# One-hot gate products with the first key as a copied, dense stationary operand, and the weights on the second key

## The chip, the cores and the metric

The kernel runs on one core of one Trainium2 chip. The metric is the device time of one execution in microseconds; the time before is the median of three runs. Engine names in the profile are PE (TensorE products), PEld (TensorE weight loads), DVE (VectorE), ACT (ScalarE), POOL (GpSimd) and SP (SyncE, which issues the DMAs).

## What is computed

The reference is one forward pass of two blocks on 256 tokens of width 1024. The last part is a layer of 16384 experts, addressed by product keys: 128 first keys times 128 second keys. Each token has 8 heads, and each head picks 16 experts, so a token has 128 pairs (first key, second key) with a weight each. Cut to what matters:

```python
# per token n: i1, i2 (128 picks each) and softmax weights g (128)
# G[n, a, b] = sum over picks of g * (i1 == a) * (i2 == b)
# y[n] = sum over a, b of G[n, a, b] * gelu(h[n] . u[a, b]) * v[a, b]
```

The kernel computes G for all 16384 experts of a token as a product of matrices on TensorE: the picks lie on the 128 partitions, one operand is the one-hot matrix of the first keys (128 picks x 128 keys), the other that of the second keys, and one of the two is multiplied by the weights. The weights are held in two fp16 parts (a high and a low one), so each token takes two products that add up in PSUM.

## The kernel before, in words

`peer` holds the layer. After the scores of the keys and the choice of the best 16 per head (`topk`), `weights` (line 1560) leaves the picks' first keys, second keys, weights' high part and low part transposed in `it` [128 picks, 4, 256 tokens], fp16. The loop over 64 expert chunks `c` (line 1618) multiplies the tokens' activations with two groups of 128 columns of `pu` per chunk (`gemm_t_chunk`, by way of `mm3`, lines 211 to 213: three products of 256 columns for each of 16 steps, all from float32r operands in two parts). Each group's weights are loaded by DMA to `raw`, copied by ScalarE to `whi` (line 206) and subtracted by VectorE to `wlo` (line 207), with three buffers each. The GELU of the result goes into `A` (lines 1637 to 1640).

From chunk 31 on (`GSTART`), the loop also calls `group` for four tokens at a time (`NT`), 64 groups over 33 chunks. `group` keeps `AHEAD` = 2 groups prepared by `spread` (line 1589). `spread` makes two tiles on VectorE, tokens innermost:

- `o` [128 picks, 2 keys, 128 values, 4 tokens]: a ramp `iof` compared with the keys (line 1594);
- `ow` [128 picks, 2 parts, 128 values, 4 tokens]: the first key's one-hot times the two weight parts (line 1595).

`group` then issues eight products (line 1607), for each token two, with `ow` of one part as the stationary operand and the second key's one-hot in `o` as the moving one. Both are read with a step of four values, since the tokens are innermost. The result [128 first keys, 128 second keys] of a token lands in a PSUM tile `t` of four buffers. VectorE multiplies it into the part of `A` that is done (line 1610), and ScalarE copies the rest into `A` (line 1612). The pool `oh` of `o` and `ow` has three buffers for each. The order on each engine is set by a scheduler with a cost model of its own, within the dependences. Afterwards the loop over `pv` multiplies `A` with the experts' outputs.

Of the kernel before, what the change touches and what calls it, by code (L numbers as in the profile page):

```python
# [43 lines left out]
def layout(inp):  # L44
    """Input arrays in the order in which the chip reads them: copies and zero padding only."""
# [16 lines left out]
    a = {}  # L62
# [90 lines left out]
class Builder:  # L153
# [19 lines left out]
    # ---------------------------------------------------------------- helpers  # L173
# [25 lines left out]
    def wchunk(self, src):  # L199
        """A chunk of weights in two exact float32r parts."""  # L200
        n = src.shape[-1]
        raw = self.wp.tile([128, n], F32, name="raw", bufs=self.raw_bufs)
        self.D.dma_start(raw, src)
        hi = self.wp.tile([128, n], F32R, name="whi")
        lo = self.wp.tile([128, n], F32R, name="wlo")
        self.S.activation(hi, raw, AF.Copy)  # L206
        self.last_lo = self.V.tensor_sub(lo, raw, hi.bitcast(F32))  # L207
        return hi, lo
# [8 lines left out]
    def warm(self, n, after=None):  # L217
        """Keeps TensorE's clock up while it waits: n products that nobody reads."""
# [11 lines left out]
    def gemm_n(self, act, src, evac, blocks=None, split=None, chunks=None):  # L230
        """Tokens on partitions, blocks of 512 features; chunks: the part of the contraction; split: the chunks in
        groups that all blocks take in turn."""
# [20 lines left out]
    def gemm_t(self, act, src, g, out, first):  # L253
        """One group of 128 features on partitions, [128, 256 tokens]."""
# [5 lines left out]
    def gemm_t_chunk(self, act, src, filling=False):  # L260
        """Two groups; filling: both follow the rows of an operand that is still being filled."""
# [12 lines left out]
    def order(self, first, then):  # L274
        """On one engine, then is issued after first."""
# [8 lines left out]
    def rsqrt(self, a):  # L284
        """a ** -0.5 on [128, n] float32, in place of a: a first guess from the bits, three Newton steps."""
# [16 lines left out]
    def fill(self, act, x, gain, ks=range(8), bias=None, k0=0):  # L302
        """x [128 tokens, 2, features] to features on partitions, times gain (plus bias), in two parts."""
# [21 lines left out]
    def square(self, x, acc, scale=1.0 / 32):  # L325
        """acc: the sum of (scale x) ** 2."""
        self.last_sq = self.S.activation(self.junk[:, 0:x.shape[-1]], x, AF.Square, scale=scale, accum_out=acc)

    def row_r(self, ss):
        """The rows' 1 / rms from two halves' sums, [128, 2 tiles, 2 halves] to [128, 2]."""  # L330
# [5 lines left out]
    def row_b(self, r, dst):  # L336
        """The rows' factors along the free axis, on all partitions, [128, 256]."""
# [24 lines left out]
    def norm_act(self, act, x, ss, gain, bias, pool):  # L362
        """Rows over their rms, times gain plus bias."""
# [11 lines left out]
    # ---------------------------------------------------------------- first block  # L375
# [15 lines left out]
    def add_x(self, ss):  # L391
        """Adds a product to x and takes the sums of squares."""
# [6 lines left out]
    def mixer1(self):  # L399
        nc, V, S, T, P = self.nc, self.V, self.S, self.T, self.P  # L400
        with self.pool("m1") as mp, self.pool("ss") as ssp, self.pool("cv") as cvp, self.pool("sbt") as sbp:
# [8 lines left out]
            with self.pool("a1") as ap:  # L410
# [56 lines left out]
                # the branches' products, each with its rows' factors  # L467
# [10 lines left out]
    def stick_pre(self, q, r, sq, sp):  # L478
        """Queries and keys, normed, a pair of heads on partitions."""
# [25 lines left out]
    def stick(self, qt, v, m, sq, sp):  # L505
        V, S, T, P = self.V, self.S, self.T, self.P
        self.act_table("natural_log_exp_and_others", self.last_s)
        # keys on partitions: masked where key >= query
# [46 lines left out]
        def end():  # L555
            """The rows' 1 / rms."""
# [10 lines left out]
    def conv_sum(self, ab, cp):  # L567
        """The depthwise convolution: the first taps on VectorE, the last on TensorE as diagonal products."""
# [63 lines left out]
    def ssm_pre(self, sp, ends):  # L632
# [13 lines left out]
        # cos and sin of theta * t, [128 states, 8, 256], t from 1 (the phase of step t is t-1 later)  # L646
# [12 lines left out]
        # discretisation  # L659
# [16 lines left out]
        # inputs' weights, a group's channels to its states; outputs' weights times the inputs' factor fr + i fi  # L676
# [21 lines left out]
    def ssm(self, u, ab, mixed, sums, sp, mag, cs, sn, pad, bl):  # L698
        V, S, T, P = self.V, self.S, self.T, self.P
        # inputs of the states, turned back by theta t, scanned, turned forth  # L700
# [44 lines left out]
    def xa_mem(self):  # L745
        """The memory, features on partitions, and its rows' 1 / rms."""
# [11 lines left out]
    def xa_k(self, q):  # L758
        """Keys of the memory."""
# [10 lines left out]
    def xa_v(self):  # L770
        """Values of the memory."""
# [4 lines left out]
    def xa_q(self, act, w, r, q):  # L776
        """Queries or keys of rows still without their factor r, and the heads' mean squares."""
# [12 lines left out]
    def xa_r(self, ss, r):  # L790
        """The heads' factors."""
# [106 lines left out]
    # ---------------------------------------------------------------- second block  # L898
    def mod(self, mp, f0, f1, after):
        """The modulation's columns: silu(c) w_mod + b_mod, [128, 48]; the context's first two parts, [128, 16]."""  # L900
# [43 lines left out]
    def gates_rows(self):  # L944
        """The modulation's last four parts as rows in DRAM."""
# [7 lines left out]
    def gate_row(self, i, dst):  # L953
        """Part i of those four on all partitions, [128, 1024]."""
# [3 lines left out]
    def mix_consts(self):  # L958
# [4 lines left out]
        # resets of the scans along tokens  # L963
# [8 lines left out]
        # keys on partitions: direction 0 keeps s <= t, direction 1 s >= t  # L972
# [20 lines left out]
    def prep_gates(self, o, act, lat, mp, tp):  # L993
        """mLSTM's gates from the projections of h (tokens of the latents or of the context)."""
        V, S, T, P = self.V, self.S, self.T, self.P
        n = "l" if lat else "c"
        # gates
# [4 lines left out]
        # log sigmoid of the forget gates, to the input gates' rows: direction 0 at 0, direction 1 at 32  # L1002
# [11 lines left out]
        def by_step(t, x, end=True):  # L1014
            """Two columns: the chunks of 128 tokens in the direction's order, or back in the tokens' order."""
# [58 lines left out]
    def prep_gla(self, o, act, lat, mp, tp):  # L1074
        """GLA's queries, keys and decays, by head: (direction, 64 channels) on partitions."""
# [4 lines left out]
        # decays' logarithms, times 16  # L1080
# [30 lines left out]
        else:  # L1111
            # down to the context's end
# [31 lines left out]
    def prep_ml(self, o, act, lat, mp):  # L1144
        """mLSTM's queries and keys: channels on partitions, convolved over three tokens."""
# [43 lines left out]
    def out_gates(self, act, gates, i):  # L1189
        """The gates on a mixer's outputs [128, 2, 512]."""  # L1190
# [83 lines left out]
    def gla_ctx(self, o):  # L1274
        """The state after the context, [128 (direction, 64 keys), head, 128 values]: a direction's first."""
# [9 lines left out]
    def gla_states(self, o):  # L1285
        """The states at the starts of the chunks of 64 tokens."""
# [504 lines left out]
```

## Time and profile before

| what | us |
|---|---|
| median of 3 runs | 1547.19 |
| lowest, highest run | 1546.6, 1550.41 |
| span of the profiled execution | 1549.8 |
| PE busy in that span | 1495.7 |
| DVE busy | 1305.8 |
| ACT busy | 824.7 |
| PE busy, 947 to 1187 us | 240.0 |
| DVE busy, 947 to 1187 us | 218.36 |
| ACT busy, 947 to 1187 us | 103.97 |

The profile is one execution on the chip. Busy time counts the instructions of an engine; a wait is put down to the instruction that ended it. Weight loads overlap products, so PE and PEld do not add up. "Idle before" in a group of instructions is the time that the engine stood still just ahead of them. The stretch from 947 to 1187 us holds the 512 products of line 1607.

### The profile page before, as it was taken

The numbers are of one execution on the slowest core, as the hardware profiler recorded it, in microseconds if no ns is written. First come the engines' busy times: TensorE is split into PE (matmuls) and PEld (weight loads), VectorE is DVE, ScalarE is ACT, GpSimd is POOL, SyncE is SP. The second block draws the span as 40 slices with busy tenths as digits, with TensorE's granted clock in tenths as the row PEclk, the third lists the DMA queues.
The fourth block names the chain that finished last, engine by engine and source line by source line (L and its number), as shares of the span: only waits on it lengthen the run. The fifth ranks groups of instructions, "written<-read, shape, count | busy, mean of one in ns | idle before, by whom it ended". The sixth has DMA issues, their size and how long they took to land.

```text
span 1549.8 us, 24779 instructions
## 1 busy us (share of the span) xinstructions
PE 1495.7 (97%) x9395; PEld 1331.7 (86%) x9395; DVE 1305.8 (84%) x2452; ACT 824.7 (53%) x1245; POOL 27.0 (2%) x34
## 2 busy tenths in 40 slices
PE   7998899999989999999999999999999999999996
PEld 7876677899977898879999999999999877887785
DVE  8989885899877767877998988888998787888788
ACT  7564666454445756645444445444444555556553
POOL 3000000000000000000000000000000000000001
PEclk9989999999999999999999999999999999999998
DMA  6630375588884553335555554444444665665553
GB/s 231 205 108 14 127 255 196 188 273 305 308 293 141 178 163 100 124 116 164 181 182 182 178 181 153 140 141 137 138 142 143 211 215 197 197 203 196 191 192 122
DMA packets 77655, 275.56 MB, mean 178 GB/s; under 512 B 8512, under 2 KB 10976, under 8 KB 76896
## 3 DMA queue, kind: packets, MB, share of 16 engines
q1 hardware_dynamic: 77536, 273.98, 53.6%
q8 instruction: 73, 1.20, 0.3%
q14 instruction: 46, 0.38, 0.1%
HBM read 271.84 MB, written 2.11 MB: 177 GB/s over the span
## 4 chain that ended last, share of the span: by engine, by line
PE 67%; DVE 15%; DMA 11%; issue 3%; ACT 3%; SPq 0%; ACTq 0%; DVEq 0%
PE g L212 17%; PE g L213 17%; PE g L211 17%; DMA raw<-in_pv 5%; PE t L1607 4%; DVE wlo L207 4%; DMA wmod<-in_w_mod 2%; ACT whi L206 2%; PE t L212 2%; PE t L213 1%; PE t L211 1%; DMA raw<-in_ffn_out 1%; DVE wmod L921 1%; DMA cc<-in_rows 1%; DVE tlo L1670 1%
## 5 line engine op out<-in xcount | busy, mean ns | idle before, releaser
L206 ACT ACTIVATE whi<-raw 128x1024 fp32r<-128x1024 f32 x420 | 443.8, 1059 | 502.4 <-PE g L212 160.3
L207 DVE TENSOR_TENSOR wlo<-raw,whi 128x1024 fp32r<-128x1024 f32 x420 | 511.2, 1221 | 112.2 <-ACT whi L206 110.0
L211 PE MATMUL g<-h2h,whi 128*128 128x256 f32 x1152 | 329.2, 286 | 0.2 <-ACT whi L206 0.2
L212 PE MATMUL g<-h2l,whi 128*128 128x256 f32 x1152 | 326.5, 284 | 0.0
L213 PE MATMUL g<-h2h,wlo 128*128 128x256 f32 x1152 | 325.4, 283 | 0.0
L211 PEld LDWEIGHTS g<-h2h,whi 128*128 128x128 f32 x1152 | 220.9, 192 | 0.8 <-ACT h2h L319 0.4
L212 PEld LDWEIGHTS g<-h2l,whi 128*128 128x128 f32 x1152 | 220.3, 191 | 0.0
L213 PEld LDWEIGHTS g<-h2h,wlo 128*128 128x128 f32 x1152 | 220.0, 191 | 0.0
L212 PE MATMUL g<-wlo,ah 128*128 128x512 f32 x328 | 126.0, 392 | 0.9 <-DVE wlo L207 0.8
L213 PE MATMUL g<-whi,al 128*128 128x512 f32 x328 | 122.9, 389 | 0.0
L211 PE MATMUL g<-whi,ah 128*128 128x512 f32 x328 | 103.3, 389 | 0.0
L211 PE MATMUL g<-hfh,whi 128*128 128x256 f32 x352 | 100.0, 285 | 3.3 <-ACT whi L206 1.9
L212 PE MATMUL g<-hfl,whi 128*128 128x256 f32 x352 | 99.5, 283 | 0.0
L213 PE MATMUL g<-hfh,wlo 128*128 128x256 f32 x352 | 98.2, 284 | 0.9 <-DVE wlo L207 0.9
L212 PEld LDWEIGHTS g<-wlo,ah 128*128 128x128 f32 x328 | 61.6, 188 | 16.1 <-DVE wlo L207 2.3
L211 PEld LDWEIGHTS g<-whi,ah 128*128 128x128 f32 x328 | 61.6, 188 | 12.9
L213 PEld LDWEIGHTS g<-whi,al 128*128 128x128 f32 x328 | 61.6, 188 | 12.6
L211 PEld LDWEIGHTS g<-hfh,whi 128*128 128x128 f32 x352 | 66.4, 189 | 5.1 <-ACT whi L206 3.2
L921 DVE SCALAR_TENSOR_TENSOR wmod<-wmod,cc 128x1024 f32<-128x1024 f32 x48 | 58.6, 1220 | 10.1 <-DMA wmod<-in_w_mod 8.2
L213 PEld LDWEIGHTS g<-hfh,wlo 128*128 128x128 f32 x352 | 65.6, 188 | 1.3 <-DVE wlo L207 1.2
L212 PEld LDWEIGHTS g<-hfl,whi 128*128 128x128 f32 x352 | 66.2, 188 | 0.0
L1607 PE MATMUL t<-o,ow 128*128 128x128 f16 x512 | 65.8, 297 | 0.0
(637 smaller groups left out, 3053.9 us busy)
## 6 DMA issues: line engine op xcount, KB each, us to landing
raw<-in_pu SPq DMA_DIRECT2D x128, 512.0 KB, 3.9
raw<-in_pv SPq DMA_DIRECT2D x128, 512.0 KB, 4.0
wmod<-in_w_mod SPq DMA_DIRECT2D x48, 512.0 KB, 5.7
raw<-in_ffn_in SPq DMA_DIRECT2D x44, 512.0 KB, 5.5
raw<-in_ffn_out SPq DMA_DIRECT2D x22, 512.0 KB, 4.5
raw<-in_w_out SPq DMA_DIRECT2D x16, 512.0 KB, 3.5
raw<-in_pwq SPq DMA_DIRECT2D x16, 512.0 KB, 4.1
raw<-in_w_qkv SPq DMA_DIRECT2D x12, 512.0 KB, 4.3
```

What stands on the lines that cost most here:

```text
L206: self.S.activation(hi, raw, AF.Copy)
L207: self.last_lo = self.V.tensor_sub(lo, raw, hi.bitcast(F32))
L211: a = self.T.matmul(out, ahi, bhi, start=start, stop=False, skip_group_check=True)
L212: self.T.matmul(out, ahi, blo, start=False, stop=False, skip_group_check=True)
L213: b = self.T.matmul(out, alo, bhi, start=False, stop=stop, skip_group_check=True)
L921: i = V.scalar_tensor_tensor(o, w, 1.0, cc[:, j], op0=OP.mult, op1=OP.mult, accum_out=acc)
L1607: T.matmul(p[:, k], w[:, i, :, k], o[:, 1, :, k], start=k + i == 0, stop=i == 1, skip_group_check=True)
L1670: V.tensor_sub(lo[:, 0:n], raw[:, 0:n], hi[:, 0:n].bitcast(F32))
```

## The change

The roles of the two keys are exchanged, and the layouts with them. `iof` shrinks to pairs of tokens. `it` holds the two keys and `wt` the two weight parts, both as [128 picks, 128 token pairs, 2, 2 tokens]. In `spread`, `o` and `ow` are [128 picks, 2 pairs, 2 keys or parts, 128 values, 2 tokens], so that two tokens are innermost. `ow` is now the second key's one-hot times the weights. ScalarE copies the first key's one-hot from `o` to a new tile `od` [128 picks, 4 tokens, 128 values], where the 128 values of one token lie side by side. The product takes `od` as the stationary operand for both parts and `ow` as the moving one, with a step of two values. `o` has two buffers in place of three. The rest of the diff removes comments.

```diff
-            self.iof = pc.tile([128, 128, NT], F16, name="iof")
-            P.iota(self.iof, pattern=[[1, 128], [0, NT]], base=0, channel_multiplier=0,
+            self.iof = pc.tile([128, 128, 2], F16, name="iof")
+            P.iota(self.iof, pattern=[[1, 128], [0, 2]], base=0, channel_multiplier=0,
...
-            it = pc.tile([128, 4, 256], F16, name="idxT")
+            it, wt = (pc.tile([128, 128, 2, 2], F16, name=n) for n in ("idxT", "wgtT"))
...
-                        V.tensor_copy(it[:, i], p)
+                        V.tensor_copy(it[:, :, i], p.rearrange("p (a t) -> p a t", t=2))
...
                         V.tensor_scalar(g, p, 32768.0, None, op0=OP.mult)
-                        V.tensor_copy(it[:, 2], g)
-                        V.tensor_sub(it[:, 3], g, it[:, 2])
+                        g = g.rearrange("p (a t) -> p a t", t=2)
+                        V.tensor_copy(wt[:, :, 0], g)
+                        V.tensor_sub(wt[:, :, 1], g, wt[:, :, 0])
...
             def spread(t0):
-                o = op[0].tile([128, 2, 128, NT], F16, name="o")
-                w = op[0].tile([128, 2, 128, NT], F16, name="ow")
-                row = lambda i: it[:, i:i + 2, None, t0:t0 + NT].to_broadcast([128, 2, 128, NT])
-                V.tensor_tensor(o, self.iof[:, None].to_broadcast([128, 2, 128, NT]), row(0), op=OP.is_equal)
-                V.tensor_mul(w, o[:, 0:1].to_broadcast([128, 2, 128, NT]), row(2))
-                ready.append((o, w))
+                n = [128, NT // 2, 2, 128, 2]
+                o = op[0].tile(n, F16, name="o", bufs=AHEAD)
+                w = op[0].tile(n, F16, name="ow")
+                d = op[0].tile([128, NT, 128], F16, name="od")
+                row = lambda z: z[:, t0 // 2:(t0 + NT) // 2, :, None].to_broadcast(n)
+                V.tensor_tensor(o, self.iof[:, None, None].to_broadcast(n), row(it), op=OP.is_equal)
+                V.tensor_mul(w, o[:, :, 1:2].to_broadcast(n), row(wt))
+                S.activation(d.rearrange("p (g t) j -> p g t j", t=2), o[:, :, 0].rearrange("p g j t -> p g t j"),
+                             AF.Copy)
+                ready.append((d, w))
...
-                o, w = ready.pop(0)
+                d, w = ready.pop(0)
...
-                        T.matmul(p[:, k], w[:, i, :, k], o[:, 1, :, k], start=k + i == 0, stop=i == 1,
+                        T.matmul(p[:, k], d[:, k], w[:, k // 2, i, :, k % 2], start=k + i == 0, stop=i == 1,
```

## Rows read from the trace of the kernel before

**Rows 1.** The page: busy time of each engine; the chain that ended last, by line.
```profile
PE 1495.7 (97%) x9395; PEld 1331.7 (86%) x9395; DVE 1305.8 (84%) x2452; ACT 824.7 (53%) x1245; POOL 27.0 (2%) x34
...
PE g L212 17%; PE g L213 17%; PE g L211 17%; DMA raw<-in_pv 5%; PE t L1607 4%; DVE wlo L207 4%; DMA wmod<-in_w_mod 2%; ACT whi L206 2%; PE t L212 2%; PE t L213 1%; PE t L211 1%; DMA raw<-in_ffn_out 1%; DVE wmod L921 1%; DMA cc<-in_rows 1%; DVE tlo L1670 1%
```

**Rows 2.** Line 1607 by itself: its weight loads and its products.
```profile
L1607 PEld LDWEIGHTS <-ow x512: 112/117/136, 947.5 to 1185.2; 128*128 128x128 f16 x171
L1607 PE MATMUL t<-o,ow x512: 282/297/303, 947.5 to 1185.3; 128*128 128x128 f16 x171
```

**Rows 3.** TensorE in order of time, 1046 to 1056 us: start, length, line, count.
```profile
1046.80 2.05 PE L1607 MATMUL t<-o,ow 128*128 128x128 f16 x16
...
1054.33 0.28 PE L213 MATMUL g<-h2h,wlo 128*128 128x256 f32 x1
1054.45 2.05 PE L1607 MATMUL t<-o,ow 128*128 128x128 f16 x16
1056.25 0.37 PE L211 MATMUL g<-h2h,whi 128*128 128x256 f32 x1
```

**Rows 4.** Busy time of the engines in four stretches of the stage: PE, PEld, DVE, ACT, POOL.
```profile
947.00:1007.00 60.00, 60.00 (x504) 59.48 (x504) 51.19 (x73) 27.79 (x47) 0.00 (x0) 1.00 0.43 136
1007.00:1067.00 60.00, 60.00 (x504) 59.49 (x503) 53.44 (x70) 26.94 (x48) 0.00 (x0) 1.00 0.42 139
1067.00:1127.00 60.00, 60.00 (x504) 59.42 (x503) 55.76 (x70) 24.41 (x47) 0.00 (x0) 1.00 0.42 139
1127.00:1187.00 60.00, 60.00 (x504) 59.42 (x503) 57.97 (x69) 24.83 (x48) 0.00 (x0) 1.00 0.43 141
```

**Rows 5.** Groups by line, 947 to 1186 us: busy, mean ns, idle before them.
```profile
L207 DVE TENSOR_TENSOR wlo<-raw,whi 128x1024 fp32r<-128x1024 f32 x63 | 77.1, 1224 | 17.2 <-ACT whi L206 16.9
L206 ACT ACTIVATE whi<-raw 128x1024 fp32r<-128x1024 f32 x63 | 67.0, 1064 | 133.7 <-issue 96.3 <-PE g L212 37.4
...
L1610 DVE TENSOR_TENSOR A<-A,t 128x256 f32<-128x256 f32 (+31 forms) x62 | 60.9, 1026 | 0.0
...
L1595 DVE TENSOR_TENSOR ow<-o,idxT 128x1024 f16<-128x1024 f16 x61 | 41.5, 688 | 0.0
L1594 DVE TENSOR_TENSOR o<-iof,idxT 128x1024 f16<-128x1024 f16 x61 | 40.9, 690 | 4.6 <-PE t L1607 4.2
```

**Rows 6.** Line 526 by itself, a product of 16-bit operands that lie dense.
```profile
L526 PEld LDWEIGHTS <-identb x16: 95/98/151, 93.6 to 138.4; 128*128 128x128 bf16 x16
L526 PE MATMUL t<-sbmask,identb x16: 219/219/314, 93.6 to 138.5; 128*128 128x128 bf16 x16
```

**Rows 7.** TensorE in order of time near 93 us: two products of line 526.
```profile
93.56 0.28 PE L526 MATMUL t<-sbmask,identb 128*128 128x128 bf16 x2
```

**Rows 8.** Lines 1513 and 1514 by themselves: VectorE on 1024 fp16 values.
```profile
L1513 DVE TENSOR_TENSOR tkz<-io,tkc x8: 673/692/696, 742.0 to 928.6; 128x1024 f16<-128x1024 f16 x8
...
L1514 DVE TENSOR_TENSOR tkz<-tkz,tkf x8: 1217/1219/1225, 744.3 to 930.8; 128x1024 f16<-128x1024 f16 x8
```

**Rows 9.** All engines in order of time, 940 to 948 us: the first groups are prepared.
```profile
940.28 1.89 DVE L1594 TENSOR_TENSOR o<-iof,idxT 128x1024 f16<-128x1024 f16 x3
...
941.74 0.58 ACT L1640 ACTIVATE A<-g 128x512 f32<-128x512 f32 x1
...
943.88 1.90 DVE L1595 TENSOR_TENSOR ow<-o,idxT 128x1024 f16<-128x1024 f16 x3
```

**Rows 10.** All engines in order of time, 1055 to 1062 us: one chunk.
```profile
1055.74 1.49 DVE L1594 TENSOR_TENSOR o<-iof,idxT 128x1024 f16<-128x1024 f16 x2
...
1059.35 1.06 ACT L206 ACTIVATE whi<-raw 128x1024 fp32r<-128x1024 f32 x1 [2.81 <-issue]
...
1060.31 0.39 ACT L1640 ACTIVATE A<-g 128x280 f32<-128x280 f32 x1
...
1062.10 0.41 PE L1607 MATMUL t<-o,ow 128*128 128x128 f16 x2
```

**Rows 11.** Line 206 by itself: ScalarE's queue waiting ahead of it.
```profile
L206 ACTq EVENT_SEMAPHORE  x62: 2382/2781/4287, 949.5 to 1180.8; - x62
```

## The prediction

> **What bounds the kernel now.** The page comes first. TensorE is busy for 97% of the span and VectorE for 84%, and in the chain that ended last the one-hot products (line 1607) have 4%, about 62 us [rows 1]. So a shorter line 1607 can matter, if nothing stands close behind TensorE where it runs. Its products start between 947.5 and 1185.2 us [rows 2], in 32 batches, one per expert chunk from chunk 31 on (the first one covers two chunks), 7.65 us apart in mid-stage [rows 3]. I call 947 to 1187 us the stage. Cut into four stretches of 60 us [rows 4], it shows TensorE full in each at a granted clock of 1.00 (its 2.4 GHz level), while VectorE climbs: 51.2, 53.4, 55.8 and 58.0 us of 60. The climb is line 1610, which grows with the chunk [rows 5]. ScalarE has 104 of 240 us. VectorE's idle time there is nearly all a wait for `whi` [rows 5], so it waits for weights that TensorE's own pace releases. TensorE bounds the stage, with VectorE 15% behind at its start and 3% behind at its end.
>
> **TensorE's part of the change.** In mid-stage a batch of 16 products starts at 1054.45, the next product of line 211 at 1056.25 [rows 3]: 1.80 us, or 112 ns per product (117 ns inside the batch, the weight load's length [rows 2]). Both operands there are read with a step of four fp16 values, 8 bytes. The nearest product with both operands dense is line 526, also 128x128 in 16 bits: 219 ns against 297, its load 98 against 117 ns [rows 2, 6], and a pair of them takes 0.28 us, so the second starts 60 ns after the first [rows 7]. The change makes the stationary operand dense and leaves the moving one a step of two fp16 values, 4 bytes. No row shows that step in 16 bits. The products of lines 211 to 213 move elements of 4 bytes side by side, 256 columns every 0.12 us [rows 3], which is 60 ns for 128. So what the array must fetch at a 4-byte pitch comes at full pace, and I take 60 ns, the value on which both rows agree. The bounds are 98 ns (loads that do not overlap, from line 526's load) and 112 ns (nothing gained). At 60 ns the saving on TensorE is 512 x 0.0525 = 26.9 us, or 6.7 us in each stretch. The number of loads and products stays: the whole span has as many loads as products [rows 1], though lines 211 and 212 share their stationary operand, so one shared by two products is loaded twice.
>
> The Trainium skill speaks against half of this. "SBUF — State Buffer" (Door 1: The DMA port swizzle, its note on cachelines) says that two hits on a 16-byte line already give full bandwidth; an 8-byte step in fp16 has two. "TensorE: Matmul & The Clock Gate" (Weight-path perf modes) lets the fast weight load read packed or strided. By these the old layout cost nothing, and that is the rival of no gain below; the 78 ns between lines 1607 and 526 speak against them here. The second page (Back-to-back issue gap) also gives 81 ns as the sustained pace at 128 columns. By it the saving on TensorE would be 512 x 0.0315 = 16 us, and the run would come out some 3 us above my number.
>
> **VectorE's part.** Per group, `o` and `ow` stay two instructions of 1024 fp16 values. Now they take 690 and 688 ns with an innermost run of four tokens [rows 5]; afterwards the run is a pair. Line 1513, with a run of 16, takes 692; line 1514, where an operand has an innermost step of zero, 1219 for the same shape [rows 8]. So the price of a pair lies between 0.69 and 1.22 us. I take 0.69, because the pair is still two adjacent values of every operand, as in line 1513 and not in 1514. The upper end is a rival. Lines 1610 and 1638 and the weights are untouched. In `weights` three casts of 256 values get outputs with gaps, once; even at the 0.69 us of four times as many values they would be 2 us, and they stand ahead of the stage, where VectorE does not set the pace.
>
> **ScalarE's part.** 64 copies of 512 values are new. The nearest row is line 1640, 128x512 in 0.58 us [rows 9]: 37 us on ScalarE, 141 of some 226. It sits idle 133.7 us before line 206 [rows 5], which covers them. What is queued behind a copy is the next `whi`; the copy waits for `o`. What waits for the copy is TensorE's batch. In a sample chunk the two `o` end at 1057.23 and the batch comes at 1062.10 [rows 10]: 4.9 us for two copies of 0.58. If they stand behind the `whi` that runs from 1059.35 and the 0.39 us after it, they end at 1061.9, with 0.2 us to spare; ahead of that `whi` they fall into its wait of 2.81 us. I cost them at nothing; without that cover the price is the rival of the late copy. The 4.2 us that `o` waits for TensorE [rows 5] go, since TensorE no longer reads `o`. At the stage's start `ow` follows 1.7 us after the last `o` [rows 9], time enough for its copies. The smaller iota is on POOL, which has 27 us of work in the whole span [rows 1].
>
> **The sum.** TensorE would need 60 - 6.7 = 53.3 us per present stretch. VectorE needs 51.2, 53.4, 55.8 and 58.0, and takes over in the last three. If it could run without a gap, the stage would be 53.3 + 53.4 + 55.8 + 58.0 = 220.5, a saving of 19.5 us. The fullest stretch that the trace shows has it at 58.0 of 60, or 96.6%. At that fill the four are 53.3, 55.3, 57.7 and 60.0, together 226.3: a saving of 13.7 us. I take the second, as it is the fill that a row shows: 14 us, half of what TensorE sheds. What is late next is VectorE, not the products. The profiled span of 1549.8 becomes 1536; it stands 2.6 us above the median of 1547.2, within the runs' 1546.6 to 1550.4, so the median becomes 1533.
>
> **Rivals.**
> - *The load sets the pace.* The product alternates with a load, and if loads of 98 ns [rows 6] do not overlap, the saving is 512 x 0.0145 = 7.4 us, TensorE stays the bound, 1540. For it: the 117 ns pace equals the load's length now. Against it: the second product of line 526 starts 60 ns after the first.
> - *No gain on TensorE.* The 112 ns come from something other than the steps, or a 4-byte step is as slow as an 8-byte one. Then 1547, give or take 3. Against it: the 78 ns and the 4-byte columns of line 211.
> - *The late copy.* ScalarE works in order, and its waits ahead of `whi` have a median of 2.8 us and reach 4.3 [rows 11]. A copy behind a long one misses the 0.2 us above, and TensorE waits. At 14 / 32 = 0.44 us per chunk the gain is gone; at 1 us per chunk the run is at 1533 + 32 = 1565, and about 1550 between.
> - *Slower: a pair breaks VectorE's pace.* If an innermost run of two drops `o` and `ow` to line 1514's 1.22 us, VectorE gets 128 x 0.53 = 68 us more: 286 us, at 96.6% 296 against 240, and the run is at 1603. It decides from 22 us on, that is, once the two take 0.86 us each. Against it: a run of four shows no loss against a run of 16.
>
> **How the numbers follow.** Forecast 0.62, with 1528 (no gap in VectorE) to 1538 as its own range; load-bound 0.13; no gain 0.10; late copy 0.08; broken pair 0.07. A measurement of this kernel tells about 0.3% (4.6 us) from no change. Faster by more: 0.62 + 0.13 + 0.01 of the late copy = 0.76. Within: 0.10 + 0.02 = 0.12. Slower: 0.07 + 0.05 = 0.12. The range from 1527 to 1549 takes in the forecast (0.59), the load-bound case (0.13), most of no gain (0.08) and a little of the late copy (0.02).
>
> **What would show it.** Right: products at line 1607's successor that start some 60 ns apart and last near 219 ns; VectorE at 96% or more of the stage from its second quarter on; TensorE with gaps for the first time there, released by `wlo` or by the copies; the stage some 226 us long; `o` and `ow` still 0.69 us. Wrong: starts 98 ns or more apart, `o` or `ow` above 0.86 us, or gaps in TensorE that end with the copy. The sum fails most easily in VectorE's fill, which no row shows without TensorE holding it back.

## The result, and the profile of the changed kernel

| | before | changed |
|---|---|---|
| median, us | 1547.04 | 1527.76 |
| lowest, highest run | 1546.6, 1550.41 | 1525.51, 1530.05 |
| span of the profiled execution | 1549.8 | 1524.2 |

The ratio is 0.9869, with a 95% interval of 0.985 to 0.9887: 20 us less, where the prediction said 14. Of the median of before 1547.2, a factor of 0.9869 is 1526.9, just under the low end of the range. A second timing, further down, gives 0.9858. So the direction was right and the gain is about one and a half times the forecast.

The page of the changed kernel, busy time of each engine and the chain by line, as in [rows 1]:

```profile
PE 1465.9 (96%) x9395; PEld 1300.3 (85%) x9395; DVE 1300.9 (85%) x2452; ACT 861.3 (57%) x1309; POOL 27.3 (2%) x34
...
PE g L211 16%; PE g L213 16%; PE g L212 16%; DMA raw<-in_pv 8%; DVE wlo L207 5%; DMA wmod<-in_w_mod 3%; ACT whi L206 2%; PE t L1614 2%; DVE tlo L1677 1%; DVE al L1667 1%; DMA raw<-in_ffn_in 1%; DVE wlo L1677 1%; PE t L212 1%; PE t L213 1%; PE t L211 1%
```

TensorE is busy 30 us less and VectorE 5 us less, ScalarE 37 us more. In the chain the one-hot products fall from 4 to 2%, and the loads of `pv` and `wlo` grow.

The products by themselves, now line 1614, to be read against [rows 2]:

```profile
L1614 PEld LDWEIGHTS <-od x512: 94/96/101, 937.1 to 1148.6; 128*128 128x128 f16 x171
L1614 PE MATMUL t<-ow,od x512: 217/219/233, 937.1 to 1148.6; 128*128 128x128 f16 x171
```

A product takes 219 ns in place of 297, its load 96 in place of 117, the same two numbers as line 526 in [rows 6]. The eight bytes' step is gone from both. Two rows in order of time at the start of the stage (start, length, engine, line, count):

```profile
933.72 1.29 DVE L1600 TENSOR_TENSOR ow<-o,wgtT 128x1024 f16<-128x1024 f16 x2
...
937.07 1.10 PE L1614 MATMUL t<-ow,od 128*128 128x128 f16 x16
```

Sixteen products take 1.10 us; less the last one's 0.22, the other fifteen start 59 ns apart. In [rows 3] the same sixteen took 2.05 us. The row above it shows two neighbouring `ow` on VectorE in 1.29 us: with 0.68 for the second, the first holds the engine for only 0.61.

The engines in stretches of the stage, as in [rows 4] (PE, PEld, DVE, ACT, POOL; the last stretch has 38 us):

```profile
937.00:997.00 60.00, 60.00 (x575) 59.53 (x575) 58.77 (x86) 42.98 (x73) 0.00 (x0) 1.00 0.49 157
997.00:1057.00 60.00, 60.00 (x568) 59.61 (x567) 58.51 (x78) 41.20 (x70) 0.00 (x0) 1.00 0.48 156
1057.00:1117.00 60.00, 60.00 (x570) 59.44 (x570) 60.00 (x75) 35.85 (x68) 0.00 (x0) 1.00 0.46 151
1117.00:1155.00 38.00, 35.86 (x334) 35.02 (x333) 37.58 (x44) 19.32 (x40) 0.00 (x0) 1.00 0.41 137
```

TensorE now gets 575, 568 and 570 products done in 60 us where it did 504, and is still full in the first three stretches. VectorE is at 58.8, 58.5, 60.0 and 37.6 of 38. The prediction's best fill, 58.0 of 60, is passed from the first stretch on.

The groups by line from the first batch to the last, as in [rows 5] (busy, mean ns, idle before them):

```profile
L207 DVE TENSOR_TENSOR wlo<-raw,whi 128x1024 fp32r<-128x1024 f32 x61 | 74.2, 1216 | 0.7 <-ACT whi L206 0.6
L206 ACT ACTIVATE whi<-raw 128x1024 fp32r<-128x1024 f32 x61 | 64.5, 1058 | 15.7 <-PE g L212 9.3 <-issue 4.3 <-DMA raw<-in_pu 0.6
L1617 DVE TENSOR_TENSOR A<-A,t 128x256 f32<-128x256 f32 (+30 forms) x60 | 58.3, 1013 | 0.0
L1600 DVE TENSOR_TENSOR ow<-o,wgtT 128x1024 f16<-128x1024 f16 x62 | 40.2, 685 | 2.0 <-PE t L1614 1.7
L1599 DVE TENSOR_TENSOR o<-iof,idxT 128x1024 f16<-128x1024 f16 x61 | 39.8, 684 | 0.0
...
L1601 ACT ACTIVATE od<-o 128x512 f16<-128x512 f16 x61 | 35.6, 618 | 0.0
```

`o` and `ow` take 684 and 685 ns, so a pair of tokens innermost costs VectorE nothing. The new copy, line 1601, takes 618 ns, with no idle time ahead of it. VectorE's 17.2 us of waiting for `whi` are 0.7 us now.

Where the time came from is best seen by cutting at the last batch. The kernel before, from the first batch to the last and the 30 us after that:

```profile
947.50:1185.30 237.80, 237.80 (x1992) 235.62 (x1991) 216.66 (x277) 103.23 (x187) 0.00 (x0) 1.00 0.43 139
1185.30:1215.30 30.00, 30.00 (x158) 25.85 (x157) 22.55 (x30) 15.34 (x23) 0.00 (x0) 1.00 0.55 176
```

And the changed one:

```profile
937.10:1148.60 211.50, 210.45 (x1998) 208.44 (x1997) 208.79 (x275) 136.25 (x243) 0.00 (x0) 1.00 0.47 153
1148.60:1178.60 30.00, 26.46 (x135) 22.45 (x133) 21.29 (x24) 14.90 (x23) 0.00 (x0) 0.94 0.51 167
```

From the first to the last batch 237.8 us become 211.5, which is 26.3 us less. In it VectorE stands still for 237.8 - 216.7 = 21.1 us before and 2.7 us afterwards. In the 30 us that follow, TensorE has no gap before, and 3.5 us of gaps afterwards. There a part is given back. The mean granted clock of that stretch is 0.94 in this profile: some 3.4 us at the lower of its two levels (1.2 GHz), behind the gaps, which costs TensorE some 1.7 us of work at the upper one.

The stretches do not hold exactly the same work. Without its 512 one-hot products, the one before has 1480 products of `pu`, the changed one 1486, and one of these takes 0.12 us [rows 3]; a difference of 1 us between two runs' batches can come from that.

### The profile page after: what moved, and what is told of

Read it like the earlier page. It is cut to its first block, busy times and chain, and to the rows that moved or that the text cites. A ratio compares the mean times of both kernels' runs of the same rounds, so it can differ in the third digit from the quotient of the medians.

```text
span 1524.2 us, 24941 instructions
## 1 busy us (share of the span) xinstructions
PE 1465.9 (96%) x9395; PEld 1300.3 (85%) x9395; DVE 1300.9 (85%) x2452; ACT 861.3 (57%) x1309; POOL 27.3 (2%) x34
## 4 chain that ended last, share of the span: by engine, by line
PE 57%; DVE 19%; DMA 14%; issue 5%; ACT 4%; SPq 0%; ACTq 0%; DVEq 0%
PE g L211 16%; PE g L213 16%; PE g L212 16%; DMA raw<-in_pv 8%; DVE wlo L207 5%; DMA wmod<-in_w_mod 3%; ACT whi L206 2%; PE t L1614 2%; DVE tlo L1677 1%; DVE al L1667 1%; DMA raw<-in_ffn_in 1%; DVE wlo L1677 1%; PE t L212 1%; PE t L213 1%; PE t L211 1%
## 5 line engine op out<-in xcount | busy, mean ns | idle before, releaser
L1617 DVE TENSOR_TENSOR A<-A,t 128x248 f32<-128x248 f32 (+31 forms) x64 | 63.3, 1032 | 0.5 <-ACT A L1647 0.5
```

The source lines that it names most:

```text
L1617: V.tensor_mul(a[:, :, 0:j0], a[:, :, 0:j0], p[:, :, 0:j0])
```

## The experiments

Two numbers of each run tell most: the stretch from the first one-hot product to the last (first and last start by the product's own line), and the rest of the span after it.

| run | first, last product | batches | span | rest |
|---|---|---|---|---|
| before | 947.5, 1185.3 | 237.8 | 1549.8 | 364.5 |
| before_again | 944.6, 1182.4 | 237.8 | 1548.3 | 365.9 |
| changed | 937.1, 1148.6 | 211.5 | 1524.2 | 375.6 |
| after_again | 939.8, 1151.3 | 211.5 | 1522.3 | 371.0 |
| after_timed | 948.8, 1160.4 | 211.6 | 1529.5 | 369.1 |
| stationary_step2 | 942.7, 1155.9 | 213.2 | 1524.0 | 368.1 |
| moving_step4 | 942.5, 1179.8 | 237.3 | 1545.9 | 366.1 |
| pairs_only | 945.8, 1159.0 | 213.2 | 1526.3 | 367.3 |
| moving_step1 | 938.7, 1152.9 | 214.2 | 1523.5 | 370.6 |
| stationary_step4 | 945.6, 1159.7 | 214.1 | 1531.1 | 371.4 |
| no_weighting | 941.7, 1152.9 | 211.2 | 1518.1 | 365.2 |
| weighting_plus_half | 944.7, 1179.3 | 234.6 | 1543.0 | 363.7 |
| low_part_on_ACT | 942.2, 1158.7 | 216.5 | 1529.7 | 371.0 |
| some_wlo_on_POOL | 942.9, 1154.9 | 212.0 | 1525.8 | 370.9 |

### Both kernels once more

No edit.

> The kernel before once more, for the spread of its parts between executions. Two theories of the 9.8 us that the loop over pv takes longer in the changed kernel's profile (368.4 against 358.6 us from the last product of pu to the end), and of the 9.7 us by which that profile is ahead when the first batch comes (937.1 against 947.5). Spread of executions: a second profile of the kernel before differs from the first by some 5 to 10 us in either part. Caused by the change: the second profile has the first batch within 2 us of 947.5 and the loop over pv within 2 us of 358.6.

> The changed kernel once more. Spread: the first batch and the loop over pv move by several us against the first profile (937.1 and 368.4), while the batches take 211 to 212 us from the first to the last product again, as that stretch is paced by TensorE. Caused by the change: 937 and 368 again, within 2 us.

The start of the first batch moves by several us from one execution to the next: 947.5 and 944.6 in the kernel before, 937.1, 939.8 and, in the third profile, 948.8 in the changed one. So the 9.7 us by which the first profile was ahead there are spread. The batches do not move: 237.8 and 237.8, 211.5, 211.5 and 211.6. The rest moves by less than the difference of the two kernels: 364.5 and 365.9 against 375.6, 371.0 and 369.1. Neither theory held for the rest as it was put. Of the 9.8 us in the first pair of profiles some is spread, but the means, 365.2 before and 371.9 in the changed kernel, leave 6.7 us for the change. Then 26.3 - 6.7 = 19.6 us is the net gain, near the 20 us of the timing.

Of the 6.7 us only a part repeats. The 30 us behind the last batch, in after_again and after_timed:

```profile
1151.30:1181.30 30.00, 26.45 (x141) 22.59 (x139) 22.64 (x26) 14.90 (x23) 0.00 (x0) 1.00 0.53 175
```

```profile
1160.40:1190.40 30.00, 26.49 (x141) 22.62 (x139) 22.62 (x26) 15.71 (x24) 0.00 (x0) 1.00 0.54 175
```

The 3.5 us of gaps are there each time. The lower clock is not: it is 1.00 in these two, with 141 products done against 135 in the first profile. So 1.7 us of the first profile's 375.6 are its clock, and in the third, 369.1, hardly anything is given back beyond the gaps.

### Which operand's step set the pace

Without ScalarE's copy, the stationary operand read straight from `o`, which has three buffers again, as in all the runs below without the copy:

```diff
-                o = op[0].tile(n, F16, name="o", bufs=AHEAD)
+                o = op[0].tile(n, F16, name="o")
...
-                d = op[0].tile([128, NT, 128], F16, name="od")
...
-                S.activation(d.rearrange("p (g t) j -> p g t j", t=2), o[:, :, 0].rearrange("p g j t -> p g t j"),
-                             AF.Copy)
-                ready.append((d, w))
+                ready.append((o, w))
...
-                        T.matmul(p[:, k], d[:, k], w[:, k // 2, i, :, k % 2], start=k + i == 0, stop=i == 1,
+                        T.matmul(p[:, k], o[:, k // 2, 0, :, k % 2], w[:, k // 2, i, :, k % 2], start=k + i == 0, stop=i == 1,
```

> The changed kernel without ScalarE's copy: the stationary operand is read straight from o with a step of two values (4 bytes), the moving one as before with a step of two. Theory A (the moving operand's 8-byte step set the old pace, the load hides): product pace stays near 58 ns and the time is that of the changed kernel within 0.3%. Theory B (the stationary operand's step set the pace, which is why a copy is needed): the load grows from 96 ns towards 117 and the pace to 75 ns or more, 512 x 0.017 = 9 us or more on TensorE's stage.

Its loads and products by themselves:

```profile
L1611 PEld LDWEIGHTS <-o x512: 96/97/101, 942.7 to 1155.8; 128*128 128x128 f16 x171
L1611 PE MATMUL t<-ow,o x512: 217/218/233, 942.7 to 1155.9; 128*128 128x128 f16 x171
```

Load and product are those of the changed kernel, 97 and 218 ns, and the ratio to the kernel before is 0.9872 (0.9832 to 0.9911), against 0.9869. So the copy brings nothing that the time shows. The batches alone are 1.7 us longer without it, 213.2 us against 211.5, with 3.4 us of gaps of TensorE in place of 1.1.

The other half: the copy and the exchanged keys, but tokens four innermost as before.

```diff
-                o = op[0].tile([128, 2, 128, NT], F16, name="o")
+                o = op[0].tile([128, 2, 128, NT], F16, name="o", bufs=AHEAD)
                 w = op[0].tile([128, 2, 128, NT], F16, name="ow")
...
-                V.tensor_mul(w, o[:, 0:1].to_broadcast([128, 2, 128, NT]), row(2))
-                ready.append((o, w))
+                d = op[0].tile([128, NT, 128], F16, name="od")
+                V.tensor_mul(w, o[:, 1:2].to_broadcast([128, 2, 128, NT]), row(2))
+                S.activation(d, o[:, 0].rearrange("p j t -> p t j"), AF.Copy)
+                ready.append((d, w))
...
-                        T.matmul(p[:, k], w[:, i, :, k], o[:, 1, :, k], start=k + i == 0, stop=i == 1,
+                        T.matmul(p[:, k], d[:, k], w[:, i, :, k], start=k + i == 0, stop=i == 1,
```

> The kernel before with the roles of the keys exchanged and ScalarE's copy, tokens still four innermost: the stationary operand dense, the moving one with the old step of four values (8 bytes). Theory A (moving step sets the pace): pace 105 to 118 ns as before, stage 230 to 238 us, time within 0.3% of the kernel before. Theory B (stationary step sets it): pace 58 to 65 ns, products of 219 ns, and the time of the changed kernel.

```profile
L1609 PEld LDWEIGHTS <-od x512: 96/115/118, 942.5 to 1179.7; 128*128 128x128 f16 x171
L1609 PE MATMUL t<-ow,od x512: 273/294/296, 942.5 to 1179.8; 128*128 128x128 f16 x171
```

With a dense stationary operand the product still takes 294 ns, the batches take 237.3 us, and the ratio is 1.0 (0.9982 to 1.0018). Theory A holds on both sides: the moving operand's step sets the pace. The load's median is 115 ns here although its operand is dense, and its shortest, 96, is the dense length, so the load's length followed the products there and did not set their pace.

Then the token pairs alone, without copy and without exchange of the keys (against the changed kernel, the lines of the copy left out):

```diff
-                V.tensor_mul(w, o[:, :, 1:2].to_broadcast(n), row(wt))
+                V.tensor_mul(w, o[:, :, 0:1].to_broadcast(n), row(wt))
...
-                        T.matmul(p[:, k], d[:, k], w[:, k // 2, i, :, k % 2], start=k + i == 0, stop=i == 1,
+                        T.matmul(p[:, k], w[:, k // 2, i, :, k % 2], o[:, k // 2, 1, :, k % 2], start=k + i == 0, stop=i == 1,
```

> Only the token pairs of the change: tokens two innermost in o and ow, but the roles as in the kernel before (ow of the first key stationary, the second key's one-hot moving) and no copy by ScalarE. Theory A (the moving operand's step is all that counts): pace 57 to 59 ns and the time of the changed kernel within 0.3%. Theory B (the exchange of the keys or the dense stationary operand adds to it): slower than the changed kernel by 0.5% or more.

```profile
L1611 PEld LDWEIGHTS <-ow x512: 95/97/101, 945.8 to 1158.9; 128*128 128x128 f16 x171
L1611 PE MATMUL t<-o,ow x512: 217/218/233, 945.8 to 1159.0; 128*128 128x128 f16 x171
```

Again 97 and 218 ns. The ratio is 0.9882 (0.9857 to 0.9908), on the same chip as 0.9858 (0.983 to 0.9887) for the changed kernel: 0.24% apart, with intervals that overlap for the most part. That is what theory A allows; theory B's 0.5% would be at the far end of the interval. In the profile its batches take 213.2 us, as those of the other kernel without the copy. Of the three parts of the change, the token pairs do the work.

Two steps that the change doesn't use. The moving operand dense:

```diff
-                        T.matmul(p[:, k], d[:, k], w[:, k // 2, i, :, k % 2], start=k + i == 0, stop=i == 1,
+                        T.matmul(p[:, k], d[:, k], d[:, k], start=k + i == 0, stop=i == 1,
```

> The changed kernel with the copied one-hot od as the moving operand too (the second key and the weights are left out of the products, VectorE still makes ow): both operands dense. If a step of two fp16 values is at full pace, the products start 57 to 59 ns apart as in the changed kernel. If the step of two still costs something, 50 to 55 ns.

```profile
L1614 PEld LDWEIGHTS <-od x512: 96/98/101, 938.7 to 1152.8; 128*128 128x128 f16 x171
L1614 PE MATMUL t<-od x512: 219/219/232, 938.7 to 1152.9; 128*128 128x128 f16 x171
```

The product takes 219 ns as with a step of two. Its starts lie 56 ns apart in the median, against 58, between the two windows expected; 2 ns for 512 products are 1 us. A step of 4 bytes is at full pace to within that. The batches do not get shorter by it: they take 214.2 us, with some 14 products of `pu` more among them and 2.5 us of gaps of TensorE.

The stationary operand with the old step of 8 bytes, in the kernel without the copy:

```diff
-                        T.matmul(p[:, k], o[:, k // 2, 0, :, k % 2], w[:, k // 2, i, :, k % 2], start=k + i == 0, stop=i == 1,
+                        T.matmul(p[:, k], o[:, k // 2].rearrange("p i j t -> p (i j t)").rearrange("p (j s) -> p j s", s=4)[:, :, k % 2], w[:, k // 2, i, :, k % 2], start=k + i == 0, stop=i == 1,
```

> The kernel without the copy, its stationary operand read with a step of four values (8 bytes) from o as the kernel before read ow (128 values out of 512, so the products are of other numbers), the moving one with a step of two. Theory A (only the moving operand's step counts): 57 to 59 ns, loads of 95 to 98 ns. Theory B (an 8-byte step also slows the load): loads of 110 ns or more and a pace of 70 ns or more.

```profile
L1611 PEld LDWEIGHTS <-o x512: 110/113/138, 945.6 to 1159.7; 128*128 128x128 f16 x171
L1611 PE MATMUL t<-ow,o x512: 217/221/254, 945.6 to 1159.7; 128*128 128x128 f16 x171
```

The load does grow, to 113 ns, as theory B said; the pace does not follow. The products take 221 ns, start 59 ns apart, and the batches take 214.1 us against 213.2. So the longer load hides almost wholly behind the products that run, though it is nearly twice as long as the products are apart.

### What bounds the stage now

VectorE relieved: the product `ow` left out (`o` has three buffers here).

```diff
-                o = op[0].tile(n, F16, name="o", bufs=AHEAD)
-                w = op[0].tile(n, F16, name="ow")
+                o = op[0].tile(n, F16, name="o")
...
-                V.tensor_mul(w, o[:, :, 1:2].to_broadcast(n), row(wt))
...
-                ready.append((d, w))
+                ready.append((d, o))
...
-                        T.matmul(p[:, k], d[:, k], w[:, k // 2, i, :, k % 2], start=k + i == 0, stop=i == 1,
+                        T.matmul(p[:, k], d[:, k], w[:, k // 2, 1, :, k % 2], start=k + i == 0, stop=i == 1,
```

> The changed kernel without the product ow (the moving operand is the second key's one-hot itself, so the weights are left out of the result): VectorE loses 64 x 0.69 = 44 us in the stage, TensorE and ScalarE keep all they do. Theory V (in the changed kernel VectorE works without a gap and its backlog at the end of the stage is what the loop over pv gives back): the stretch from the first to the last batch stays at 211 to 212 us, TensorE's idle time after it falls from 21 to 22 us to the 15 to 16 us of the kernel before, and the run takes 1527.8 - 6 = 1521 to 1523. Theory D (the loop over pv is slower for its DMAs, whatever VectorE does): idle time stays at 21 us or more and the run at 1527.

From the first batch to the last, and the 30 us behind it, as above:

```profile
941.70:1152.90 211.20, 211.20 (x2010) 209.82 (x2010) 180.95 (x217) 146.21 (x248) 0.00 (x0) 1.00 0.48 157
1152.90:1182.90 30.00, 29.91 (x158) 25.63 (x156) 22.58 (x30) 16.23 (x23) 0.00 (x0) 1.00 0.58 185
```

With 181 us of work in place of 209, VectorE stands still for 30 us, and the batches are no shorter: 211.2 us against 211.5. So TensorE's own pace sets them in the changed kernel, to within the 1 us of its gaps there (12 products of `pu` more lie in this run's stretch, 1.4 us). But its gaps after the last batch are gone, 0.1 us in place of 3.5, and the rest of the span is 365.2, the value of the kernel before. Theory V holds for these gaps: they come from VectorE's backlog. The ratio to before is 0.9803 (0.9771 to 0.9835). On the value of its own chip's kernel before, 1550.8, the 20 us of the change grow to 30, while the profiles and the expectation say 6 to 7 more; the two intervals leave room for that, and the difference is not settled.

VectorE loaded: `ow` made twice in every second group.

```diff
+                if t0 % (2 * NT) == 0:
+                    V.tensor_mul(w, o[:, :, 1:2].to_broadcast(n), row(wt))
                 V.tensor_mul(w, o[:, :, 1:2].to_broadcast(n), row(wt))
```

> The changed kernel with the product ow made twice in every second group: VectorE gains 32 x 0.69 = 22 us in the stage, nothing else changes. Theory V (VectorE bounds the changed kernel from the first batch on or soon after): the time rises by 18 to 22 us, back to 1546 to 1550. If TensorE still bounded it with VectorE 3% behind: by 22 - 6 = 16 us or less, 1543 or below.

```profile
944.70:1179.30 234.60, 219.08 (x2034) 214.51 (x2033) 233.83 (x313) 142.40 (x251) 0.00 (x0) 0.97 0.45 148
```

The stretch takes 234.6 us, VectorE is busy for 233.8 of them, and TensorE has 15.5 us of gaps. But it is not the same stretch as in the other runs: it holds 36 products more of `pu`. The scheduler has set the order anew, and the last 48 one-hot products now come behind the last product of `pu`. Cut there:

```profile
944.70:1163.10 218.40, 214.81 (x1991) 210.62 (x1990) 218.31 (x293) 137.35 (x238) 0.00 (x0) 1.00 0.46 152
1163.10:1179.30 16.20, 4.27 (x47) 3.89 (x45) 15.52 (x21) 5.05 (x13) 0.00 (x0) 0.60 0.30 99
```

Up to the end of `pu` VectorE has no gap, and TensorE stands still for 3.6 us. In the 16 us behind it TensorE works for 4.3 us and waits for `ow` for 12, and its granted clock falls to 0.60. So VectorE has no room left for the extra work, and what it can't do in time is paid behind the products of `pu`. The ratio is 0.9969 (0.9952 to 0.9987), some 16 us above the changed kernel (0.010 to 0.011 of 1547). That is between the two windows, at the edge of the one for a TensorE that is 3% ahead. The expectation priced the extra product at its length, 0.69; by the row of two neighbouring `ow` it holds the engine for 0.61, so 32 of them are 19.5 us, and of these 2.7 us fit into the idle time that VectorE had left: 16.8. That this meets the 16 us is not shown to be more than chance, since the new order and the lower clock are in the 16 too.

### Two ways to relieve VectorE

The changed kernel, timed on the chip of these runs, with no edit:

> The changed kernel, timed on the chip of the three that follow: 0.987 of the kernel before, as in the first comparison.

The ratio is 0.9858 (0.983 to 0.9887).

The low part's weighting on ScalarE, in the kernel without the copy (`wlf` is the low part in float32, `wt` the high part alone):

```diff
-                V.tensor_mul(w, o[:, :, 1:2].to_broadcast(n), row(wt))
+                m = [128, NT // 2, 128, 2]
+                V.tensor_mul(w[:, :, 0], o[:, :, 1], wt[:, t0 // 2:(t0 + NT) // 2, None].to_broadcast(m))
+                for k in range(NT):
+                    S.activation(w[:, k // 2, 1, :, k % 2], o[:, k // 2, 1, :, k % 2], AF.Copy,
+                                 scale=wlf[:, t0 // 2 + k // 2, k % 2:k % 2 + 1])
```

> The kernel without the copy, with the weights' low part multiplied by ScalarE, one token at a time (256 copies of 128 values with a scale, some 0.28 us each by the 128-value forms of line 1619: 72 us), and only the high part by VectorE (0.42 us in place of 0.69, 17 us less). Theory V (VectorE is the bound by a few us and what it lacks is given back in the loop over pv): TensorE's idle time after the last batch falls to 16 us, time 4 to 7 us below the changed kernel. If ScalarE's order delays whi instead, TensorE gets gaps in the stage and the time is that of the changed kernel or above.

The copies by themselves, and who waits for whom from the first batch to the last (us, times, longest):

```profile
L1604 ACT ACTIVATE ow<-o,wlf x256: 402/427/449, 939.8 to 1157.1; 128x128 f16<-128x128 f16 x128
```

```profile
DVE wlo L207 <- ACT whi L206: 20.9, 28, 1.2
```

0.9891 (0.9868 to 0.9914), no better and rather worse. A copy of 128 values with a scale per partition takes 427 ns and not the estimated 0.28 (line 1619's copies of 128 values, which the estimate names, take 404 ns in the changed kernel's trace), so 256 of them put 109 us on ScalarE. VectorE is relieved, but it now waits 20.9 us for `whi` behind those copies: the wait of [rows 5] is back, with another cause.

Some of `wlo` on GpSimd:

```diff
-        self.last_lo = self.V.tensor_sub(lo, raw, hi.bitcast(F32))
+        self.last_lo = (self.P if pool else self.V).tensor_sub(lo, raw, hi.bitcast(F32))
...
-                p = self.gemm_t_chunk(act, self.I["pu"][c])
+                p = self.gemm_t_chunk(act, self.I["pu"][c], pool=c >= 44 and c % 2 == 0)
```

> The kernel without the copy, with one of the two wlo of chunks 44, 46 to 62 made by GpSimd in place of VectorE (10 x 1.22 = 12 us less on VectorE, late in the stage where it is fullest). Theory V: TensorE's idle time after the last batch falls to 16 or 17 us and the time is 3 to 6 us below the changed kernel. If GpSimd takes VectorE's reads away or is late with its 2.5 us (twice the 1.27 us that the 128x512 product of line 1751 takes): VectorE's other instructions get longer in those chunks, and the time is no better.

GpSimd's part of line 207 by itself, from 1030 to 1160 us (nine of the ten):

```profile
L207 POOL TENSOR_TENSOR wlo<-raw,whi x9: 2397/2612/3872, 1035.0 to 1145.2; 128x1024 fp32r<-128x1024 f32 x9
```

VectorE's groups from 1060 to 1120 us in this kernel:

```profile
L207 DVE TENSOR_TENSOR wlo<-raw,whi 128x1024 fp32r<-128x1024 f32 x13 | 15.9, 1222 | 0.5 <-ACT whi L206 0.3
L1599 DVE TENSOR_TENSOR ow<-o,wgtT 128x1024 f16<-128x1024 f16 x18 | 14.5, 805 | 0.0
L1598 DVE TENSOR_TENSOR o<-iof,idxT 128x1024 f16<-128x1024 f16 x16 | 10.8, 716 | 0.0
```

And in the changed kernel (after_timed) in the same stretch:

```profile
L207 DVE TENSOR_TENSOR wlo<-raw,whi 128x1024 fp32r<-128x1024 f32 x16 | 19.3, 1209 | 0.0
...
L1599 DVE TENSOR_TENSOR o<-iof,idxT 128x1024 f16<-128x1024 f16 x18 | 11.5, 678 | 0.0
L1600 DVE TENSOR_TENSOR ow<-o,wgtT 128x1024 f16<-128x1024 f16 x16 | 10.2, 677 | 0.0
```

0.986 (0.9836 to 0.9885), the same as the changed kernel. GpSimd takes 2.6 us for a `wlo`, up to 3.9, and VectorE's own instructions get longer beside it: `ow` 805 ns against 677, `o` 716 against 678 (676 and 675 in the kernel without the copy, stationary_step2, in the same stretch). With 18 and 16 of them this is 2.9 us, most of what the three `wlo` fewer (13 against 16, 1.22 us each) take off VectorE in that stretch. No version that computes the same beats the changed kernel beyond its interval.

## Why the prediction was right in direction and short in size

**TensorE's part was right.** It put the new pace at 60 ns; the profile has 58 to 59. It put the gain on TensorE at 26.9 us; the batches are 26.3 us shorter. The reason it gave, that elements at a 4-byte pitch come at full pace while 8 bytes halve it, is what the runs show: a moving step of 8 bytes gives 294 ns with a dense stationary operand, a step of 4 bytes gives 218 with and without one. It left open which of the two operands mattered; it is the moving one (an 8-byte step of the stationary one costs the batches 0.9 us, 214.1 against 213.2).

The rule that the prediction weighed, from the Trainium skill's "SBUF — State Buffer" (Door 1, the note on cachelines), would have two fp16 values per 16-byte line at full bandwidth. For TensorE's moving operand the measurement decides against it: two values per line cost 297 and 294 ns, four values 219. For the stationary operand its consequence holds in effect, since the 113 ns load of an 8-byte step hides. The 81 ns that "TensorE: Matmul & The Clock Gate" (Back-to-back issue gap) gives for a stream of loads and products at 128 columns were not seen: 56 to 59 ns here.

**VectorE's and ScalarE's prices per instruction were right.** 0.69 us for `o` and `ow` became 0.684 and 0.685. The copy, put at 0.58, took 0.62, and TensorE never waited for it: the rival of the late copy did not come, with no gap of TensorE released by a copy. The rival of the broken pair did not come either, nor that of the load's pace. One reading was too strong: VectorE's idle time in the stage is not nearly all a wait for `whi`; that is 17 of 22 us, and 4 were the wait of `o` for TensorE [rows 5].

**The step that failed is the term of the sum for VectorE's fill.** The sum filled VectorE to 96.6% where it takes over, because that was the fullest stretch a row showed, and so kept 13.7 us of the 26.9. But [rows 4] show VectorE while TensorE held it back; a fill seen there is what VectorE was left to do, not what it can do. Measured, it is 208.8 of 211.5 us, 98.7%, and 60.0 of 60 in the third stretch. The other end that the prediction named, no gap at all, gave 19.5 us, and the net gain is 20.

That this end meets the 20 is in part luck, for it is not the stage that got shorter by 20. Without a gap the sum still has VectorE pace three of the four stretches and the stage 220.5 us long; measured, 26.3 us of the 240 are gone, which leaves 213.7. The batches got the whole 26.3, and it was TensorE that set their pace: with 28 us less of VectorE's work, in the run without `ow`, they take 211.2 us in place of 211.5. VectorE did 208.8 us between the first and the last batch, against 216.7 before. Some 5 of these 8 us are instructions that no longer fall between the two (the lengths of those that do add up to 230.6 us, against 235.8), and some 3 come from neighbours, which overlap where no gap parts them (0.61 us for an `ow` of 0.68). Its last product into `A` ends later behind the last batch than before. In the kernel before, the last two of line 1610, start and length in order of time:

```profile
1187.53 2.63 DVE L1610 TENSOR_TENSOR A<-A,t 128x504 f32<-128x504 f32 x2 [0.25 <-ACT A L1640]
```

and in the changed kernel, the last two of line 1617:

```profile
1155.19 2.47 DVE L1617 TENSOR_TENSOR A<-A,t 128x504 f32<-128x504 f32 x2 [0.25 <-ACT A L1647]
```

That is 1190.2 - 1185.3 = 4.9 us behind the last batch before, and 1157.7 - 1148.6 = 9.1 us now. The loop over `pv` starts with a `wlo` and an `A` that come late (who waits for whom on TensorE's loads, 1148 to 1178 us):

```profile
PEld g L211 <- ACT ah L1666: 2.7, 1, 2.7
...
PEld g L213 <- DVE wlo L207: 1.3, 1, 1.3
```

The prediction cut time into fixed stretches and took the slower engine in each. It had no place for work that an engine carries over the end of the stage, so it could see neither the full gain inside nor the part given back behind. Of the 6.7 us given back, 3.5 us are TensorE's gaps in the first 30 us, the same in all three profiles, and the run without `ow` shows that they come from VectorE. The other 3 us are a mean over profiles that differ by more (375.6, 371.0 and 369.1), with 1.7 us of lower clock in the first; whether the change causes them stays open.

"TensorE with gaps for the first time, released by `wlo`" came, but only 1 us of it before the last batch. The stage of some 226 us did not come. "Half of what TensorE sheds" is wrong: three quarters stay.

## What to carry to other kernels

Read TensorE's pace from the moving operand's step first: fp16 values 8 bytes apart cost two times the pace of values 4 bytes apart, while the stationary operand's step was hidden. An operand with two of the outer index innermost keeps VectorE's pace and TensorE's. And when the bound is lifted, fill the next engine to its whole time and let it lag into the next stage: its busy share under the old bound is no limit. Before two stretches of different runs are compared, count what lies in them: an edit can move work across their ends.

## What the runs showed of the hardware

- Moving operand, 128 fp16 columns: 219 ns a product and 56 ns apart when dense, 218 to 219 and 57 to 59 apart at a step of 4 bytes, 294 to 297 and 116 to 118 apart at 8 bytes.
- Stationary operand, 128 x 128 fp16: a load of 96 to 98 ns dense or at 4 bytes, 113 ns at 8 bytes, and the products 57 to 59 ns apart all the same beside a moving step of 4 bytes.
- VectorE's two-operand products of 1024 fp16 values take 0.68 us with runs of two and 0.69 with runs of four; two neighbours take 1.29.
- ScalarE takes 427 ns for 128 fp16 values with a scale per partition, against 618 ns for 512 without one.
- A GpSimd subtraction of 1024 float32 values takes 2.6 us and goes with longer fp16 products of VectorE beside it, in the mean of a stretch 677 to 805 ns for `ow` and 678 to 716 for `o`.
- TensorE's granted clock fell to its lower level (1.2 GHz) for some 3.4 us behind the 3.5 us of gaps in one profile of the changed kernel, and stayed at 2.4 GHz behind the same gaps in two others.
